# A decoder layer in three-pass fp32r on one core: another order for seven products, background sums on GpSimd's queue, and a norm factor by token columns

## The chip, the core and the metric

The kernel runs on one core of a Trainium2 chip. The metric is device time in microseconds of one execution, inputs and outputs in device memory. All weights and activations are float32.

## What is computed

The reference is one inference step of a one-layer hybrid decoder. A prompt of 1024 tokens and eight samples of 8 tokens each (1088 tokens in all, width 1024) go through the same weights.

```python
def layer(x, ...):
    h = rmsnorm(x, norm_mix)
    q, k, v, gu, gv, ga, gb = split_in(h @ w_in)
    o  = windowed attention with sinks(q, k, v)          # window 128, 16 heads, 4 kv heads
    vn = layernorm(gelu(gv)) ; s = spatial_gating(gelu(gu), vn, ws, bs)
    merged = sigmoid(ga) * (o @ w_pa) + sigmoid(gb) * (s @ w_pb)
    x = x + merged @ w_out
    f, nconv = conv_ffn(rmsnorm(x, norm_ffn), w_up, conv_w, conv_b, w_down, conv_prev)
    return x + f, ...
def conv_ffn(h, w_up, conv_w, conv_b, w_down, prev):
    z = h @ w_up                                          # 1024 -> 2 x 2816
    c = conv_b + sum(concatenate([prev, z])[:, j:j + T] * conv_w[j] for j in range(3))
    a, b = split(c, 2)
    return (gelu(a) * b) @ w_down, ...
```

A final RMSNorm follows; the caches, the last rows of z and the normalised v rows are outputs too.

## The kernel before

**Numbers.** Every float32 operand is split into a high part (rounded to fp32r) and a low part (`split`: ScalarE's copy `wh`, VectorE's difference `wl`), and each product is three fp32r matmuls: high x high, high x low, low x high. So every weight tile costs a load on SyncE's queue (`wraw`), a cast on ScalarE and a subtraction on VectorE before TensorE can use it. The class `Weights` does this: `load` issues the loads in order on SyncE, `emit` the splits some units ahead, `get` hands the next unit to TensorE.

**Stages.** Tokens are columns, in two groups: group 0 has 576 (the samples and 512 of the prompt), group 1 has 512. Both go one after the other through projection, attention (`sc_p`, `tr_p`, `pv_p`, with gate products as filling: `fill`), gated MLP, merge and `w_out` (`x1_tile`, which also sums the squares for the next norm into `nacc` by GpSimd's additions). Group 0 ends at about 479 us of the trace, group 1 at 893. Then come the up-projection with the convolution (893 to 1400) and the down-projection.

**The up-projection by seven products.** For an output block f the two halves of w_up (rows a: a11, a12; rows b: a21, a22, each 512 of the 1024 inputs) and the two halves of the tokens make a 2 x 2 by 2 x 2 product, done with seven products instead of eight. On the weights' side four sums are needed, s1 = a21 + a22, s2 = s1 + a11, s4 = s2 + a12, s3 = a11 + a21 (the tokens' side carries the signs), made by GpSimd (`total`, tiles `ws`); on the tokens' side four differences (`combine`, and `t1_pieces` for group 1). `Chain.product(j, w)` does product j of one group into a PSUM place (`bank`) named by the letter j of `"adadaca"`: place `a` is continued three times, so what stands in it is copied out by ScalarE in between (`keep`: k1, ku, kn), `d` twice, `c` once. `za` and `zb` are the two output blocks.

**Who does what when.** The first FEW = 4 blocks are done for group 0 alone (893 to 953), while the tokens' side of group 1 is made (`rstd_last`, then the pieces of `t1_pieces`). The loop over `order` then does 18 blocks for both groups and, in between, those four for group 1 alone. For the first four blocks the weight sums are made ahead, as a background job in group 1's projection: `weight_sums` loads tiles `hx`, GpSimd adds into `ht`, and the result goes to device memory (`swd`). `half_sums` does the same for group 0's token side in group 1's attention, as an item of `fill` at every third slot (`x1d` in, `t0d` out).

**The order of the work.** The program is written in one order, and a planner (the tile framework) puts each engine's instructions into a queue by its own costs: an instruction that is ready may stand ahead of one that comes before it in the program. On the chip each queue runs strictly in its order. SyncE's queue holds all loads and stores.

Lines the text speaks of: L39 and L40 `split`, L121 the weight load, L151 `total`, L206 `mm3`, L328 and L1003 the reciprocals of the two norms before the up-projection, L348 and L936 the sums of squares, L431 and L451 the background loads, L454 to L457 the weight sums, L458 their store, L496 the scaling of a query tile, L926 `x1_tile`, L1000 to L1003 `rstd_last`, L1067 and L1069 `keep`, L1082 the products, L1093 to L1103 the results, L1110 to L1112 the convolution.

Of the kernel before, what the change touches and what calls it, by code (L numbers as in the profile page):

```python
# [15 lines left out]
P = 128  # L16
# [17 lines left out]
def layer(tc, a):  # L34
# [11 lines left out]
    with ExitStack() as top:  # L46
# [25 lines left out]
        class Weights:  # L72
# [70 lines left out]
            def total(self, name):  # L143

                if name not in self.sums:
# [4 lines left out]
                    t = self.sm.tile([P, 4, P], F32, name="ws", bufs=3)  # L150
                    G.tensor_add(t, x, y)  # L151
# [77 lines left out]
        with ExitStack() as ph1:  # L229
# [135 lines left out]
            for gr in groups:  # L365
# [57 lines left out]
                def half_sums(kk):  # L423
# [3 lines left out]
                    def loads():  # L427
                        x2, t4 = pair_of_tiles()
                        st["x"], st["t"] = x2, t4.rearrange("p (j c) -> p j c", j=4)
                        for e in range(2):  # L430
                            nc.sync.dma_start(x2[:, 576 * e:576 * e + 576], x1d[0][kk + 4 * e])  # L431

                    def sums():
# [6 lines left out]
                        nc.sync.dma_start(t0d[kk][:, 0], halves[0])  # L440
                        nc.sync.dma_start(t0d[kk][:, 1:5], st["t"])
                        nc.sync.dma_start(t0d[kk][:, 5:7], xs[1].rearrange("p (h c) -> p h c", h=2))
                    return loads, sums

                def weight_sums(f, h):

# [3 lines left out]
                    for e in range(2):  # L450
                        nc.sync.dma_start(q[:, e], wt(UP0 + f + e * NFF).rearrange(  # L451
                            "p (q h k) c -> p q h k c", q=2, h=2)[:, :, h])
                    (a11, a12), (a21, a22) = (q[:, 0, 0], q[:, 0, 1]), (q[:, 1, 0], q[:, 1, 1])
                    G.tensor_add(t[:, 0], a21, a22)  # L454
                    G.tensor_add(t[:, 1], t[:, 0], a11)
                    G.tensor_add(t[:, 2], t[:, 1], a12)
                    G.tensor_add(t[:, 3], a11, a21)  # L457
                    nc.sync.dma_start(swd[f][:, :, 2 * h:2 * h + 2], t)  # L458
# [32 lines left out]
                for c in range(2, KD):  # L491
# [8 lines left out]
                    if g == 1:  # L500
                        weight_sums(c // 2 - 1, c % 2)
# [54 lines left out]
                w = W.get()  # L556
                for i, (name, lo) in enumerate(toks):
# [342 lines left out]
                if g == 1:  # L900
                    W.sm = right(tops, "sm")
# [96 lines left out]
        def rstd_last():  # L998
            ps = psu.tile([P, 512], F32, name="st")
            PE.matmul(ps, ones, nacc, start=True, stop=False)  # L1000
            PE.matmul(ps, ones, late["sq"], start=False, stop=True)
            S.activation(nacc, ps, AF.Sqrt, bias=eps, scale=1.0 / D)
            V.reciprocal(nacc, nacc)  # L1003

        def t1_pieces():
# [6 lines left out]
            def norm(k):  # L1012
                V.scalar_tensor_tensor(x1g[k], x1g[k], gains[:, 1, k:k + 1], nacc, ALU.mult, ALU.mult)
# [42 lines left out]
        class Chain:  # L1056
# [15 lines left out]
            def product(self, j, w):  # L1072
                name = "adadaca"[j]
                first = name not in self.bank
                if first:
# [3 lines left out]
                for kk in range(4):  # L1079
                    th, tl = (x[:, (0, 1, 2, 6, 3, 5, 4)[j]] for x in tx[self.g][kk])  # L1080
# [3 lines left out]
                kept = self.kept  # L1084
                if j == 0:
# [3 lines left out]
                elif j == 2:  # L1089
                    self.keep("u", ps)  # L1090
                elif j == 3:
# [292 lines left out]
```

## Time and profile before

| | |
|---|---|
| three runs | 1683.12 us (median), 1682.99, 1685.64 |
| the profiled execution | 1680.17 us, span 1678.5 us, mean granted clock 0.989 |
| TensorE busy | 97% of the span, 10912 matmul records |
| VectorE, ScalarE, GpSimd busy | 62%, 46%, 26% |
| chain that ended last | TensorE 73%, VectorE 9%, GpSimd 6%, DMA 5%, ScalarE 4% |

The profile is one execution; the three runs are others of the same program. "Busy" of TensorE includes matmuls that run at a lowered clock, and matmuls overlap, so the count of matmuls in a window says more than the busy share. In the rows, PE is TensorE, PEld its weight loads, DVE VectorE, ACT ScalarE, POOL GpSimd, SPq SyncE's queue; "x2 | 1.0, 592" is two records, 1.0 us busy, 592 ns each on average; "[1.45 <-ACT kn L1069]" is idle time and what ended it. A row of waits has the time in total, the number of waits and the longest.

### The profile page before, as it was taken

The page shows a single profiled execution, that of the slowest core. Times are in us where ns is not written, and L with a number is a line of the kernel's source. Part 1 is how long each engine was busy: PE and PEld are TensorE (multiplying, and loading weights), DVE is VectorE, ACT ScalarE, POOL GpSimd, SP SyncE. Part 2 cuts the span into 40 slices and gives each one's busy share as a digit, 9 for nine tenths or more (in the row PEclk, how much of TensorE's full clock was granted, in tenths as well). Part 3 has the DMA queues.
Part 4 walks back from the last instruction along what each step waited for, and adds up shares of the span by engine and source line. Part 5 has one row for each costly group of instructions (what it writes and reads, how often), then busy time and mean ns, then how long its engine had stood idle before and what let it go on. Part 6 is the DMA issues. An engine that isn't in the chain of part 4 may idle for free.

```text
span 1678.5 us, 27712 instructions
## 1 busy us (share of the span) xinstructions
PE 1620.8 (97%) x10912; PEld 1507.6 (90%) x10912; DVE 1044.2 (62%) x1437; ACT 773.9 (46%) x1501; POOL 437.1 (26%) x526
## 2 busy tenths in 40 slices
PE   8999999999998999999999999899999999999997
PEld 8989999999976788898878899898998999999886
DVE  8546863644466678565466676868768768355433
ACT  6435653343343465444344555555555546344232
POOL 1302330100451434210012263635536530000001
PEclk9999999999999999999999999999999999999998
DMA  5332223244765522324473523223223227754421
GB/s 191 117 115 80 86 96 119 63 137 145 237 219 187 188 95 94 126 95 129 154 245 125 187 76 111 102 87 115 78 97 101 93 80 239 272 157 133 151 96 55
DMA packets 96179, 221.19 MB, mean 132 GB/s; under 512 B 10416, under 2 KB 24816, under 8 KB 96048
## 3 DMA queue, kind: packets, MB, share of 16 engines
q1 hardware_dynamic: 95904, 219.40, 39.6%
q8 instruction: 86, 1.41, 0.4%
q14 instruction: 45, 0.37, 0.1%
q10 hardware_dynamic: 144, 0.01, 0.0%
HBM read 177.54 MB, written 43.80 MB: 132 GB/s over the span
## 4 chain that ended last, share of the span: by engine, by line
PE 73%; DVE 9%; POOL 6%; DMA 5%; ACT 4%; issue 3%; SPq 1%; DVEq 0%; POOLq 0%; ACTq 0%
PE mm L206 29%; PE st L1082 20%; PE dn L1196 15%; PE mm L552 5%; DVE wl L40 2%; POOL ws L151 2%; DMA wraw<-wt 2%; DMA hx<-wt 1%; PE po L760 1%; PE sc L712 1%; ACT s L727 1%; DVE c L1111 1%; DMA hx<-x1d 1%; ACT wh L39 1%; PE pt L737 1%
## 5 line engine op out<-in xcount | busy, mean ns | idle before, releaser
L206 PE MATMUL mm<-hm,wh 128*128 128x320 f32 (+2 forms) x1920 | 432.5, 333 | 15.6 <-DVE stg L496 6.5
L40 DVE TENSOR_TENSOR wl<-wraw,wh 128x512 fp32r<-128x512 f32 (+3 forms) x314 | 287.9, 932 | 175.6 <-ACT wh L39 171.8
L39 ACT CAST wh<-wraw 128x512 fp32r<-128x512 f32 (+3 forms) x314 | 232.1, 755 | 349.8 <-PE mm L206 120.8
L1082 PE MATMUL st<-th,wh 128*128 128x288 f32 (+1 forms) x1232 | 362.1, 294 | 21.6 <-ACT k L1067 10.9
L1082 PE MATMUL st<-th,wl 128*128 128x288 f32 (+1 forms) x1232 | 359.4, 292 | 2.5 <-DVE wl L40 2.5
L1082 PE MATMUL st<-tl,wh 128*128 128x288 f32 (+1 forms) x1232 | 359.7, 292 | 0.0
L206 PEld LDWEIGHTS mm<-hm,wh 128*128 128x128 f32 x1920 | 303.3, 190 | 46.9 <-issue 8.3
L206 PE MATMUL mm<-hm,wl 128*128 128x320 f32 (+1 forms) x960 | 265.1, 330 | 0.0
L1082 PEld LDWEIGHTS st<-th,wh 128*128 128x128 f32 x1232 | 237.2, 193 | 26.7 <-ACT k L1067 14.0
L1196 PE MATMUL dn<-gr,wh 128*128 128x288 f32 (+3 forms) x1088 | 252.9, 324 | 0.0
L1082 PEld LDWEIGHTS st<-th,wl 128*128 128x128 f32 x1232 | 237.0, 193 | 3.6 <-DVE wl L40 3.5
L1082 PEld LDWEIGHTS st<-tl,wh 128*128 128x128 f32 x1232 | 237.2, 193 | 0.3 <-issue 0.2
L1196 PEld LDWEIGHTS dn<-gr,wh 128*128 128x128 f32 x1088 | 183.1, 188 | 13.9
L1196 PE MATMUL dn<-gr,wl 128*128 128x288 f32 (+3 forms) x544 | 175.8, 323 | 0.0
L206 PEld LDWEIGHTS mm<-hm,wl 128*128 128x128 f32 x960 | 159.6, 190 | 14.5
L1196 PEld LDWEIGHTS dn<-gr,wl 128*128 128x128 f32 x544 | 102.3, 188 | 6.9
L552 PE MATMUL mm<-w2h,hm 128*128 128x256 f32 x576 | 104.6, 283 | 1.7 <-DVE stg L537 1.4
L552 PEld LDWEIGHTS mm<-w2h,hm 128*128 128x128 f32 x576 | 89.8, 191 | 2.4 <-DVE stg L537 1.6
L206 PE MATMUL mm<-qo,wh 128*128 128x320 f32 (+2 forms) x384 | 84.6, 328 | 0.2 <-DVE stg L856 0.2
L552 PE MATMUL mm<-w2l,hm 128*128 128x256 f32 x288 | 81.4, 283 | 0.3 <-DVE w2l L40 0.3
L1111 DVE SCALAR_TENSOR_TENSOR c<-z,cw,c 128x1104 f32<-128x1104 f32 x44 | 71.1, 1620 | 14.6 <-ACT c L1110 14.5
L1229 POOL TENSOR_TENSOR x<-x,rb 128x320 f32<-128x320 f32 (+2 forms) x14 | 12.4, 912 | 260.3 <-PE dn L1196 160.2
(223 smaller groups left out, 2400.9 us busy)
## 6 DMA issues: line engine op xcount, KB each, us to landing
wraw<-wt SPq DMA_DIRECT2D x146, 512.0 KB
wraw<-wt SPq DMA_DIRECT2D x114, 256.0 KB
gd<-z SPq DMA_DIRECT2D x22, 544.0 KB
wraw<-sd SPq DMA_DIRECT2D x32, 256.0 KB
graw<-gd SPq DMA_DIRECT2D x22, 288.0 KB
wraw<-wpb SPq DMA_DIRECT2D x16, 384.0 KB
graw<-gd SPq DMA_DIRECT2D x22, 256.0 KB
gate<-stg SPq DMA_DIRECT2D x16, 288.0 KB
```

What stands on the lines that cost most here:

```text
L39: S.copy(hi, src)
L40: V.tensor_sub(lo, src, hi.bitcast(F32))
L151: G.tensor_add(t, x, y)
L206: PE.matmul(ps[:, lo:lo + c1 - c0], u[:, k, :], v[:, c0:c1], start=(k == 0 and i == 0), stop=(k == nk - 1 and i == 2))
L552: PE.matmul(ps, u[:, lo:lo + P], v[:, k, :], start=(k == 0 and i == 0), stop=(k == KD - 1 and i == 2))
L712: PE.matmul(ps[:, h, o0:256], q, kst[kv][:, e, k0:cur + P], start=e == 0, stop=e == 1)
L727: S.activation(s[:, h], s[:, h], AF.Exp, bias=nm[:, h:h + 1], accum_out=dn[:, h:h + 1])
L737: PE.transpose(pt[:, h * P:h * P + P], s[:, h, 0:P], ident)
L760: PE.matmul(po, vst[b + d][:, kv, :], t, start=e == 0, stop=e == len(parts) - 1)
L1082: PE.matmul(ps, u[:, kk, :], v, start=first and kk + i == 0, stop=kk == 3 and i == 2, skip_group_check=True)
L1111: V.scalar_tensor_tensor(c, z[:, 1:1105], cw[:, i, 1:2], c, ALU.mult, ALU.add)
L1196: PE.matmul(ps, u[:, c, :], v[:, lo:hi], start=f + i == 0, stop=f == NFF - 1 and i == 2, skip_group_check=True)
```

## The change

- **Order of the seven products.** The letters become `"adcadca"`: between two products into the same place stand two others. The weight units follow: a11, s1, a12, s2, s4, a22, s3. Places are started at j = 0, 1, 2 and again, for `c`, at 5. The last two results are now made after product 6: ScalarE copies place `a` negated, VectorE subtracts place `c` from it, GpSimd subtracts k5. Before, ScalarE wrote one of them straight from PSUM and GpSimd the other after product 4. `total("s4")` makes s3 as well, so `ws` has four buffers.
- **Background sums.** The loads of `half_sums` and the loads and the store of `weight_sums` are issued on GpSimd's DMA queue. `weight_sums` gives back its additions as a function, which `next_sums` calls one step later, ahead of the next loads. `half_sums` has its stores as a third item, and `fill` takes an item at every second slot.
- **`rstd_last`.** The sum over the width is taken by token columns (eight matmuls of one column), so square root and reciprocal run on 128 x 4 instead of 128 x 512. Then four matmuls of `ones` with `ident` scaled by a column spread the factors over all partitions again; they stay in PSUM, where `norm` reads them.
- **Memory.** The pools `bt`, `sm` and `w2` change places at the start of block 3 instead of after it.

```diff
@@ total
-                    t = self.sm.tile([P, 4, P], F32, name="ws", bufs=3)
+                    t = self.sm.tile([P, 4, P], F32, name="ws", bufs=4)
                     G.tensor_add(t, x, y)
                     self.sums[name] = t
+                    if name == "s4":
+                        self.total("s3")
@@ emit
-                            src = (lambda: t[:, 0:4], lambda: self.total("s1"),
+                            src = (lambda: t[:, 0:4], lambda: self.total("s1"), lambda: t[:, 4:8],
                                    lambda: self.total("s2"), lambda: self.total("s4"),
-                                   lambda: self.total("s3"), lambda: t[:, 4:8],
-                                   lambda: tb[:, 4:8])[j]()
+                                   lambda: tb[:, 4:8], lambda: self.total("s3"))[j]()
...
-                    for x in (wa[:, 0:4], *(swd[f][:, j] for j in range(4)), wa[:, 4:8], wb[:, 4:8]):
+                    ws = [swd[f][:, j] for j in range(4)]
+                    for x in (wa[:, 0:4], ws[0], wa[:, 4:8], ws[1], ws[2], wb[:, 4:8], ws[3]):
@@ half_sums
-                            nc.sync.dma_start(x2[:, 576 * e:576 * e + 576], x1d[0][kk + 4 * e])
+                            G.dma_start(x2[:, 576 * e:576 * e + 576], x1d[0][kk + 4 * e])
...
-                        nc.sync.dma_start(t0d[kk][:, 0], halves[0])
+
+                    def stores():
+                        nc.sync.dma_start(t0d[kk][:, 0], st["x"][:, 0:288])
                         nc.sync.dma_start(t0d[kk][:, 1:5], st["t"])
...
-                    return loads, sums
+                    return loads, sums, stores
@@ weight_sums
                     for e in range(2):
-                        nc.sync.dma_start(q[:, e], wt(UP0 + f + e * NFF).rearrange(
+                        G.dma_start(q[:, e], wt(UP0 + f + e * NFF).rearrange(
                             "p (q h k) c -> p q h k c", q=2, h=2)[:, :, h])
...
-                    nc.sync.dma_start(swd[f][:, :, 2 * h:2 * h + 2], t)
+                    def sums():
...
+                        G.dma_start(swd[f][:, :, 2 * h:2 * h + 2], t)
+                    return sums
+
+                def next_sums(i):
+                    if g == 1:
+                        if i:
+                            late["sums"]()
+                        late["sums"] = weight_sums(i // 2, i % 2) if i < 2 * FEW else None
...
-                    if g == 1:
-                        weight_sums(c // 2 - 1, c % 2)
+                    next_sums(c - 2)
...
-                    if g == 1:
-                        weight_sums(FEW - 1, kc)
                     w = W.get()
                     ps = acc2()
                     mm3(ps, chunks, w, hs, 0, KD, KD)
+                    next_sums(KD - 2 + kc)
...
                 w = W.get()
+                next_sums(KD)
...
-                    if extra and slots["at"] % 3 == 0:
+                    if extra and slots["at"] % 2 == 0:
...
-                    W.sm = right(tops, "sm")
@@ rstd_last
-            ps = psu.tile([P, 512], F32, name="st")
-            PE.matmul(ps, ones, nacc, start=True, stop=False)
-            PE.matmul(ps, ones, late["sq"], start=False, stop=True)
-            S.activation(nacc, ps, AF.Sqrt, bias=eps, scale=1.0 / D)
-            V.reciprocal(nacc, nacc)
+            ps, rt = psu.tile([P, 512], F32, name="st"), up.tile([P, 4], F32, name="rt", bufs=1)
+            for i in range(4):
+                for x in (nacc, late["sq"]):
+                    PE.matmul(ps[:, i:i + 1], x[:, i * P:i * P + P], ones[:, 0:1], start=x is nacc,
+                              stop=x is not nacc)
+            S.activation(rt, ps[:, 0:4], AF.Sqrt, bias=eps, scale=1.0 / D)
+            V.reciprocal(rt, rt)
+            rs = psu.tile([P, 512], F32, name="st")
+            for i in range(4):
+                S.activation(nacc[:, i * P:i * P + P], ident, AF.Copy, scale=rt[:, i:i + 1])
+                PE.matmul(rs[:, i * P:i * P + P], ones, nacc[:, i * P:i * P + P], start=True, stop=True)
+            return rs
...
-                V.scalar_tensor_tensor(x1g[k], x1g[k], gains[:, 1, k:k + 1], nacc, ALU.mult, ALU.mult)
+                V.scalar_tensor_tensor(x1g[k], x1g[k], gains[:, 1, k:k + 1], rs_last, ALU.mult, ALU.mult)
@@ product
-                name = "adadaca"[j]
-                first = name not in self.bank
-                if first:
+                name = "adcadca"[j]
+                first = j in (0, 1, 2, 5)
+                if name not in self.bank:
...
-                    th, tl = (x[:, (0, 1, 2, 6, 3, 5, 4)[j]] for x in tx[self.g][kk])
+                    th, tl = (x[:, (0, 1, 5, 2, 6, 4, 3)[j]] for x in tx[self.g][kk])
...
                 elif j == 2:
+                    put(self.za, 0, V.tensor_add, kept["1"], ps)
+                elif j == 3:
                     self.keep("u", ps)
...
                 elif j == 4:
+                    put(self.za, 1, V.tensor_add, kept["u"], ps)
+                elif j == 6:
                     self.keep("n", ps, -1.0)
...
-                else:
-                    for to, lo, hi in z_parts(self.zb, self.g, 0):
-                        S.activation(to, pick(ps, to, lo, hi), AF.Copy, scale=-1.0)
+                    put(self.zb, 0, V.tensor_sub, kept["n"], self.bank["c"])
+                    put(self.zb, 1, G.tensor_sub, kept["n"], kept["5"])
@@ the first FEW blocks
         for f in range(FEW):
+            if f == FEW - 1:
+                while rest:
+                    rest.pop(0)()
+                bto.close()
+                W.sm = pool2("sm", 1)
+                W.extend(pool2("w2", 1), 1)
...
-                    rstd_last()
+                    rs_last = rstd_last()
...
-        for go in rest:
-            go()
-        bto.close()
-        W.extend(pool2("w2", 1), 1)
```

More of the change, by code (lines that the diff above doesn't have):

```diff
@@ L439, in sums @@
                         combine(st["t"], *halves)
[L440 removed]
+                    def stores():
+                        nc.sync.dma_start(t0d[kk][:, 0], st["x"][:, 0:288])
                         nc.sync.dma_start(t0d[kk][:, 1:5], st["t"])
[L442 to L443 removed]
+                        nc.sync.dma_start(t0d[kk][:, 5:7], st["x"][:, 576:1152].rearrange(
+                            "p (h c) -> p h c", h=2))
+                    return loads, sums, stores
                 def weight_sums(f, h):
@@ L450, in weight_sums @@
                     for e in range(2):
-                        nc.sync.dma_start(q[:, e], wt(UP0 + f + e * NFF).rearrange(
+                        G.dma_start(q[:, e], wt(UP0 + f + e * NFF).rearrange(
                             "p (q h k) c -> p q h k c", q=2, h=2)[:, :, h])
[L453 to L458, printed above, removed]
+                    def sums():
+                        (a11, a12), (a21, a22) = (q[:, 0, 0], q[:, 0, 1]), (q[:, 1, 0], q[:, 1, 1])
+                        G.tensor_add(t[:, 0], a21, a22)
+                        G.tensor_add(t[:, 1], t[:, 0], a11)
+                        G.tensor_add(t[:, 2], t[:, 1], a12)
+                        G.tensor_add(t[:, 3], a11, a21)
+                        G.dma_start(swd[f][:, :, 2 * h:2 * h + 2], t)
[5 more added lines that the diff above has]
+                        late["sums"] = weight_sums(i // 2, i % 2) if i < 2 * FEW else None
                 def q_tile(c, f):
@@ L1084, in product, with put @@
                 kept = self.kept
+                def put(z, half, op, x, y):
+                    for to, lo, hi in z_parts(z, self.g, half):
+                        op(to, pick(x, to, lo, hi), pick(y, to, lo, hi))
                 if j == 0:
```

8 lines of the change are left out of this document (removed).

## The prediction

> **What bounds the kernel now.** I read the page's busy shares first, then the 40 us windows, then the lists of waits (TensorE, SyncE), then the timelines at the places where the windows sag.
>
> ```profile
> PE 1620.8 (97%) x10912; PEld 1507.6 (90%) x10912; DVE 1044.2 (62%) x1437; ACT 773.9 (46%) x1501; POOL 437.1 (26%) x526
> ```
>
> TensorE is the bound, and the change takes no product away, so a gain can only come from time in which TensorE stands still or runs below its pace. The windows (columns: window, length, busy and count of PE, PEld, DVE, ACT, POOL, granted clock, DMA share, GB/s) show where:
>
> ```profile
> 440.00:480.00 40.00, 36.94 (x271) 35.98 (x270) 12.24 (x11) 13.09 (x20) 26.23 (x24) 1.00 0.75 249
> 960.00:1000.00 40.00, 36.37 (x275) 35.88 (x274) 27.04 (x33) 19.31 (x39) 24.80 (x23) 0.96 0.31 105
> 1000.00:1040.00 40.00, 40.00 (x320) 40.00 (x320) 25.46 (x33) 20.25 (x42) 12.37 (x23) 1.00 0.28 92
> 1040.00:1080.00 40.00, 34.54 (x260) 33.69 (x260) 33.65 (x36) 21.05 (x41) 25.62 (x23) 0.96 0.37 127
> 1160.00:1200.00 40.00, 37.31 (x288) 36.22 (x288) 33.54 (x37) 21.35 (x43) 24.04 (x23) 1.00 0.26 94
> 1240.00:1280.00 40.00, 37.20 (x288) 37.00 (x286) 26.64 (x34) 20.69 (x41) 14.24 (x21) 0.96 0.36 116
> 1280.00:1320.00 40.00, 38.63 (x307) 38.42 (x306) 35.02 (x36) 21.23 (x42) 24.61 (x23) 1.00 0.30 101
> ```
>
> Three stages sag: the start of the second group (440 to 560), the first four output blocks (893 to 953), and the main loop over output blocks (953 to 1400).
>
> **Part 1, the order of the seven products.** An undisturbed window of the main loop holds 320 matmuls, 0.125 us each. The other five lack 45 + 60 + 32 + 32 + 13 = 182, so 22.8 us are lost. TensorE's waits name the cause:
>
> ```profile
> PE st L1082 <- ACT k L1067: 10.9, 10, 2.8
> PE st L1082 <- ACT ku L1067: 5.3, 3, 2.4
> PE st L1082 <- ACT kn L1069: 3.3, 3, 1.4
> 917.34 0.40 PE L1082 MATMUL st<-th,wh 128*128 128x288 f32 x1 [1.45 <-ACT kn L1069]
> 919.89 0.61 PE L1082 MATMUL st<-th,wl 128*128 128x288 f32 x1 [1.88 <-DVE wl L40]
> ```
>
> In sixteen waits, 19.5 us, a matmul that continues a PSUM bank waits until ScalarE has copied the bank out. Three of them lie before 953 (the 1.45 us row and two of about half a microsecond), which leaves 17 us for the main loop. ScalarE is no slow engine (46%); its queue is held:
>
> ```profile
> 1168.24 0.62 ACT L39 CAST wh<-ws 128x512 fp32r<-128x512 f32 x1 [1.41 <-POOL ws L151]
> 1169.88 0.35 ACT L1067 COPY k<-st 128x256 f32<-128x256 f32 x1
> 1170.28 0.39 PE L1082 MATMUL st<-th,wh 128*128 128x256 f32 x1 [1.50 <-ACT k L1067]
> ```
>
> The weight splits stand in ScalarE's queue ahead of the copy and wait for GpSimd's sums. The old order continues bank `a` after one other product. The new one (a d c a d c a) puts two between, and spreads the four sum splits over units 1, 3, 4 and 6 instead of 1 to 4. One product of both groups is 24 matmuls, 24 x 0.125 = 3.0 us, more than the longest wait (2.8). In the four blocks with one chain only it is half of that, so some waits shorten and don't end. I take the 17 us of named idle and leave the other 5.8 (pipeline refill, low clock), for what remains; ends -22.8 and -5 (rival 2).
>
> What it costs: the last result changes from a ScalarE copy to a VectorE subtraction out of PSUM. Its nearest rows are the additions of the same shapes:
>
> ```profile
> 953.20:1400.50 447.30, 430.10 (x3361) 426.40 (x3361) 332.73 (x383) 234.72 (x466) 218.91 (x243) 0.99 0.29 98
> L1100 DVE TENSOR_TENSOR z<-k,st 128x256 f32<-128x256 f32 x22 | 9.2, 417 | 11.4 <-PE st L1082 11.4
> L1100 DVE TENSOR_TENSOR z<-k,st 128x224 f32<-128x224 f32 x18 | 6.8, 379 | 0.0
> L1100 DVE TENSOR_TENSOR z<-k,st 128x64 f32<-128x64 f32 x18 | 3.9, 217 | 23.7 <-PE st L1082 23.7
> ```
>
> That is 9.2 + 6.8 + 3.9 = 19.9 us more for VectorE, which is busy 332.73 of 447.3 us; its 114 us of idle cover it, so zero (without that cover, 19.9). Queued behind the subtraction are weight splits, which here run ahead of their product. GpSimd's subtraction moves from the fifth product to the last; what follows it is the convolution of that block, which TensorE doesn't read. The fourth `ws` buffer is memory only. **Part 1: -17.**
>
> **Part 2, the background sums leave SyncE's queue.** The largest single stall is here. The chain in order of time, then the waits of SyncE (427 to 516) and the clock:
>
> ```profile
> 512.89 0.57 SPq L458
> ...
> 515.21 0.42 SPq L121
> ...
> 515.72 6.07 DMA wraw<-wt
> ...
> 525.59 3.75 DVE nacc L328
> 530.03 1.19 PE L206 MATMUL mm<-hm,wh 128*128 128x512 f32 x2 [6.55 <-DVE stg L496]
> SPq L458 <- POOL ht L456: 34.2, 6, 7.0
> 530.00:532.00 2.00, 1.97 (x5) 1.61 (x6) 1.94 (x3) 1.95 (x3) 0.00 (x0) 0.50 0.02 2
> 532.00:534.00 2.00, 2.00 (x8) 1.57 (x7) 1.97 (x3) 0.24 (x1) 0.00 (x0) 0.71 0.79 260
> ```
>
> SyncE's queue waits for GpSimd's sum to store it (34.2 us in six waits), and the kernel's own weight load at 515.21 stands behind. TensorE idles 6.55 us and then runs four microseconds at 0.50 and 0.71, another 1.0 + 0.6. With loads and stores on GpSimd's queue that weight load can go some 7 us earlier, about the whole stall: -8.1. Next late is the reciprocal (3.75 us) ahead of L496, while TensorE has a second accumulator to fill, so I count nothing for it. The 40 - 36.94 = 3 us idle at 440 to 480 I leave as they are: there the `stg` buffers come free by GpSimd's additions (the L348 row below), and GpSimd gets no faster.
>
> GpSimd pays: 8 steps x 3 issues = 24 DMAs; no row shows one from this queue.
>
> ```profile
> L451 SPq DMA_DIRECT2D hx<-wt x16: 551/616/1020, 427.4 to 505.9; - x16
> 427.00:513.00 86.00, 82.19 (x502) 73.16 (x501) 47.07 (x50) 35.22 (x50) 48.82 (x50) 1.00 0.66 216
> L348 POOL TENSOR_TENSOR pacc<-pacc,stg 128x512 f32<-128x512 f32 x7 | 9.9, 1418 | 0.2
> ```
>
> Bounds: SyncE's 0.616 us for the same transfer, and 6.07 us if the queue were held until a load lands. I take 0.62, the same instruction on another queue: 24 x 0.62 = 15 us, inside GpSimd's idle 86 - 48.8 = 37.2. Behind a waiting sum stand the additions for `nacc` and `pacc`, which free `stg` and feed the second group's norm; that is so today. The row also shows that the planner starts these loads at 427, long before their place in the program, so the new hooks (`next_sums`) fix a dependency more than a time. In attention GpSimd gets eight x1 loads, 8 x 0.62 = 5 us, among masks that TensorE needs: 0 to +5, and as they are spread over the stage I take +1. `stores` one slot later takes SyncE's wait for VectorE away there, worth nothing that TensorE shows. **Part 2: -8 + 1 = -7.**
>
> By the Trainium skill (DMA: Bandwidth & Descriptors, Issuing engines are not separate DMA queues) all issuers share the same DMA engines, and a second one saves only issue time; by that rule this part would be zero (rival 1). The 34.2 us row speaks against it: what is saved is a wait in the queue, not an issue.
>
> **Part 3, rstd_last and the first four blocks.**
>
> ```profile
> 902.00:920.40 18.40, 15.07 (x110) 14.55 (x109) 17.77 (x25) 9.29 (x21) 7.75 (x10) 0.96 0.23 77
> 902.01 3.35 DVE L1003 RECIPROCAL nacc<-nacc 128x512 f32<-128x512 f32 x1
> 577.80 0.18 DVE L729 RECIPROCAL dn<-dn 128x4 f32<-128x4 f32 x1 [1.78 <-ACT s L727]
> 920.00:922.00 2.00, 2.00 (x9) 2.00 (x10) 2.00 (x4) 0.00 (x0) 0.46 (x1) 0.50 0.39 134
> 924.00:926.00 2.00, 1.77 (x8) 1.42 (x6) 1.65 (x4) 1.46 (x4) 1.03 (x1) 0.58 0.89 224
> L1002 ACT ACT_TABLE_LOAD x1 | 1.3, 1283 | 1.1 <-PE st L1001 1.1
> L1000 PE MATMUL st<-nacc,c_ones 128*128 128x512 f32 x2 | 1.0, 592 | 0.0
> L361 PE MATMUL pt<-c_ones,pacc 128*128 128x1 f32 x18 | 2.1, 241 | 0.0
> L737 PE MATMUL pt<-c_ident,s 128*128 128x128 f32 x128 | 19.2, 272 | 0.7 <-DVE s L730 0.6
> ```
>
> VectorE is full here (17.77 of 18.4), and TensorE's two stalls (1.45 + 1.88 = 3.3) and the low clock after them (three windows from 920 to 926, the first and last shown, 0.50, 0.50 and 0.58: 2.8 us) follow from it. The reciprocal falls from 3.35 to 0.18: -3.2 on VectorE; the new subtractions give back 0.6 per block, about 1. Net 2.2 of the 3.3 go, and I take most of the clock loss with them: -5; the two half-microsecond bank waits, -1. New on TensorE (each fp32 matmul stands as two records): eight of one column, 16 x 2.1 / 18 = 1.9, and four of 128, 8 x 19.2 / 128 = 1.2, for two of 512, 2 x 1.0: about +1. The four wait for square root, reciprocal and four ScalarE copies in order; TensorE's queue may stand for the table load (1.3) and as much again, 0 to 3 us, or the planner puts products ahead of them: +1. The earlier close of `bt` and the `sm` and `w2` pools touch nothing that is late: zero, with products of block 3 as cover. **Part 3: -4** (-7 to +3).
>
> **Sum.** -17 - 7 - 4 = -28 on the profiled execution's 1680.17 (span 1678.5): 1652. The median of the runs, 1683.12, lies 2.95 above it, so 1655.
>
> **Rivals.**
> 1. *The queue was not the cause.* Weight loads are late because the DMA engines are busy (share 0.75 at 440 to 480) and stay late. Part 2 gives +1, the sum -20: 1663. Against it: the load was issued late, not only landed late.
> 2. *The wait moves to the weights.* With the banks free, TensorE meets the splits that wait for GpSimd. Part 1 gives -5, the sum -16: 1667. For it: the L39 row above waits 1.41 us for a sum. Against: the sixteen waits name copies only.
> 3. *GpSimd's queue becomes the bound (slower).* Each issue holds GpSimd for x us. Idle covers 37.2 / 24 = 1.55; beyond that `pacc` and the buffers come late by 24x - 37.2, and TensorE's norm with them. Against the other parts' 20 it decides from x = 2.4. At 3.3, the middle of 0.62 and 6.07: 42 - 20 = +22, so 1705. For it: the 26.23 of 40 us GpSimd already works at 440 to 480. Against: at SyncE's issue price there is room. The Trainium skill (SBUF — State Buffer, A bandwidth-pool intuition that's wrong) tells of a transfer from this queue that takes about 3.1 us instead of 0.62 beside a VectorE copy, which would make 1700, as an estimate; no run here shows it yet.
> 4. *It does not do what it says.* The planner rearranges all queues and the waits reappear elsewhere: no change.
>
> **How the numbers follow.** Forecast 0.48, rival 1 0.17, rival 2 0.13, rival 3 0.17, rival 4 0.05. Predicted 1655. The forecast's best end, -22.8 - 8 - 7 and no cost, gives 1645; rivals 1 and 2 together with part 3 at zero give 1680; part of rival 3 and of rival 4 reach 1688. The range is 1644 to 1688, with most of rival 3 left out. 0.2% is 3.4 us, about what a measurement of this kernel can tell from no change. Faster 0.48 + 0.17 + 0.13 = 0.78, same 0.05, slower 0.17.
>
> **What would show it.** Part 1 right: waits on `k`, `ku`, `kn` after the first blocks under 4 us, main loop windows near 320; wrong: waits on `wh`, `wl` or `ws` in their place. Part 2 right: no stall of 6 us between the second group's query products, and SyncE's wait for `ht` gone; wrong: GpSimd's DMA rows longer than 1.55 us, or `pacc` late at the norm. Part 3 right: no reciprocal of 3 us at about 900, and no half clock after it; wrong: a wait of TensorE at the four diagonal matmuls. The prediction as a whole is wrong if the time is over 1680.

## The result, and the profile after

The changed kernel takes 1705.51 us (median of four runs, 1704.60 to 1708.48), the kernel before 1684.38 in the same comparison: a ratio of 1.0127, 95% interval 1.0109 to 1.0145. It is slower by 21 us; the forecast was 1655, the range ended at 1688, and the outcome is rival 3's side and almost its number. The profiled execution took 1708.48 us, the longest of the four; its span is 1706.8. The profile of before is a short execution (1680.17; other runs of that kernel lie between 1678.2 and 1690.8). So the two spans differ by 28 us where the medians differ by 21, and a few microseconds between two traces mean nothing.

Where the time went is seen from the starts of the stages, each the first or last row of its kind in the timeline of TensorE (us):

| | group 0's last product | group 1's values | up-projection | main loop | down-projection | span |
|---|---|---|---|---|---|---|
| before | 477.8 | 548.4 | 893.3 | 954.5 | 1400.3 | 1678.5 |
| after | 509.3 | 576.8 | 928.5 | 986.0 | 1426.5 | 1706.8 |
| part 2 alone (e2) | 510.9 | 578.0 | 927.4 | 987.6 | 1433.6 | 1712.2 |
| parts 1 and 3 (e11) | 478.0 | 553.6 | 897.9 | 952.6 | 1392.2 | 1672.2 |

After is 31 us late by the end of group 0 and 28 to 35 us late until the up-projection; between the starts of the up- and the down-projection it wins 9 back. (Between group 1's values and the first transpose another 6 us are lost, 3.75 of them a wait of the value projection for VectorE that was 1.37 in before; no experiment follows that part.) Busy time by engine, from the page of after, and then its windows in the lost stage, in the columns of before's:

```profile
PE 1626.9 (95%) x10932; PEld 1514.6 (89%) x10932; DVE 1046.5 (61%) x1503; ACT 756.8 (44%) x1439; POOL 445.2 (26%) x558
```

```profile
440.00:480.00 40.00, 23.94 (x152) 23.51 (x151) 5.11 (x5) 7.58 (x11) 22.02 (x26) 0.79 0.47 159
480.00:520.00 40.00, 29.21 (x158) 25.66 (x158) 12.71 (x14) 9.59 (x14) 27.55 (x28) 0.83 0.55 180
```

TensorE's busy time is that of before but for 6 us, so 22 of the 28 us are idle. The first window holds 152 matmuls where before had 271. GpSimd is busy for 22 of 40 us, less than the 26 of before, and the DMA share fell from 0.75 to 0.47: nothing is full, so this is waiting. Who waits for whom (lists of waits of after: TensorE, then GpSimd and SyncE between 425 and 560):

```profile
PE mm L207 <- DVE stg L939: 25.8, 4, 13.1
PE st L1103 <- ACT k L1088: 7.0, 7, 2.2
...
PE st L1103 <- DVE z L1109: 4.5, 3, 1.7
...
POOL hx L457 <- issue: 20.7, 7, 3.7
POOL ht L462 <- DMA hx<-wt: 17.9, 6, 5.9
...
SPq L341 <- POOL nacc L949: 21.9, 3, 7.5
```

The longest of TensorE's waits for L939 can be followed in the timelines of after (GpSimd, then VectorE and TensorE); L457 is the background load, L462 to L465 the sums, L466 their store, L949 the `nacc` addition, L939 `x1_tile`, L341 the load of a piece of x:

```profile
436.81 0.77 POOL L466 DMA_DIRECT2D sd<-ht  x1 [0.42 <-POOL ht L464]
437.51 0.72 POOL L457 DMA_DIRECT2D hx<-wt  x1
441.87 0.72 POOL L457 DMA_DIRECT2D hx<-wt  x1 [3.64 <-issue]
448.51 0.73 POOL L462 TENSOR_TENSOR ht<-hx 128x256 f32<-128x256 f32 x1 [5.92 <-DMA hx<-wt]
...
452.50 0.71 POOL L457 DMA_DIRECT2D hx<-wt  x1
455.52 0.72 POOL L457 DMA_DIRECT2D hx<-wt  x1 [2.31 <-issue]
458.85 0.71 POOL L462 TENSOR_TENSOR ht<-hx 128x256 f32<-128x256 f32 x1 [2.61 <-DMA hx<-wt]
...
460.89 1.39 POOL L949 TENSOR_TENSOR nacc<-nacc,stg 128x576 f32<-128x576 f32 x1
462.31 0.75 DVE L939 TENSOR_TENSOR stg<-stg,mm 128x576 f32<-128x576 f32 x1 [16.51 <-POOL nacc L949]
463.20 1.30 PE L207 MATMUL mm<-hm,wh 128*128 128x320 f32 x4 [13.15 <-DVE stg L939]
```

A store and the first load of the next step go out in 0.7 us each; the second load waits 3.64 us for something the trace does not name ("issue"). Then the queue stands for the landing. The first `nacc` addition stands two such steps behind, amid the sums of a third. It frees the `stg` tile, without which VectorE can't empty TensorE's accumulator. The last two of the four waits go one step further round: the addition that begins at 483.19 frees the tile, SyncE issues the load of x into it at 484.62, and VectorE waits until that has landed. SyncE's 21.9 us for `nacc` (7.8 in before) are waits of this kind. In the timeline of before the same addition started 16 us earlier:

```profile
445.04 1.43 POOL L936 TENSOR_TENSOR nacc<-nacc,stg 128x576 f32<-128x576 f32 x1 [0.45 <-ACT stg L935]
```

### The profile page after: what moved, and what is told of

Its sections match the earlier page's. It is cut to its first block, busy times and chain, and to the rows that moved or that the text cites. A ratio compares the mean times of both kernels' runs of the same rounds, so it can differ in the third digit from the quotient of the medians.

```text
span 1706.8 us, 27748 instructions
## 1 busy us (share of the span) xinstructions
PE 1626.9 (95%) x10932; PEld 1514.6 (89%) x10932; DVE 1046.5 (61%) x1503; ACT 756.8 (44%) x1439; POOL 445.2 (26%) x558
## 4 chain that ended last, share of the span: by engine, by line
PE 67%; DVE 9%; POOL 8%; DMA 6%; issue 5%; ACT 4%; SPq 0%; DVEq 0%; POOLq 0%; ACTq 0%
PE mm L207 26%; PE st L1103 17%; PE dn L1219 15%; PE mm L565 5%; POOL ws L151 2%; DMA wraw<-wt 2%; DVE wl L40 2%; DMA hx<-wt 1%; ACT s L741 1%; PE po L774 1%; PE sc L726 1%; DMA hx<-x1d 1%; ACT wh L39 1%; POOL z L1109 1%; DMA traw<-t0d 1%
## 5 line engine op out<-in xcount | busy, mean ns | idle before, releaser
L207 PE MATMUL mm<-hm,wh 128*128 128x320 f32 (+2 forms) x1920 | 438.0, 337 | 37.7 <-DVE stg L939 25.8
L207 PEld LDWEIGHTS mm<-hm,wh 128*128 128x128 f32 x1920 | 308.4, 193 | 69.4 <-DVE stg L939 13.7
L1132 DVE SCALAR_TENSOR_TENSOR c<-z,cw,c 128x1104 f32<-128x1104 f32 x44 | 66.3, 1508 | 46.6 <-ACT c L1131 46.6
L1131 ACT ACTIVATE c<-z,cw 128x1104 f32<-128x1104 f32 x44 | 57.7, 1311 | 73.0 <-DVE z L1109 40.1
```

The lines of the kernel that those rows point to most:

```text
L207: PE.matmul(ps[:, lo:lo + c1 - c0], u[:, k, :], v[:, c0:c1], start=(k == 0 and i == 0), stop=(k == nk - 1 and i == 2))
L1131: S.activation(c, z[:, 2:1106], AF.Identity, bias=cw[:, i, 3:4], scale=cw[:, i, 2:3])
L1132: V.scalar_tensor_tensor(c, z[:, 1:1105], cw[:, i, 1:2], c, ALU.mult, ALU.add)
```

## The experiments

The theory (Q): GpSimd's in-order queue carries work that TensorE waits for (`nacc`, `pacc`), and part 2 put transfers in front of it that stand. Rivals: the transfers crowd the DMA engines wherever they are issued; the loss comes from the other parts. Every run is given as its ratio to the kernel before, timed beside it, with the run's own median. Differences to the kernel before are the ratio's, times 1684; differences between changed kernels are of medians.

**Which part (e1 to e4, e11).** e1 is the changed kernel with the transfers back on SyncE:

```diff
-                            G.dma_start(x2[...], x1d[0][kk + 4 * e])
+                            nc.sync.dma_start(x2[...], x1d[0][kk + 4 * e])
...
-                        G.dma_start(q[:, e], wt(...)...)
+                        nc.sync.dma_start(q[:, e], wt(...)...)
...
-                        G.dma_start(swd[f][:, :, 2 * h:2 * h + 2], t)
+                        nc.sync.dma_start(swd[f][:, :, 2 * h:2 * h + 2], t)
```

> The changed kernel with all 24 background transfers (loads of half_sums, loads and stores of weight_sums) back on SyncE's queue; everything else as changed, next_sums too. Theory Q (GpSimd's own queue is the cause: it stands while it issues transfers, and the nacc and pacc additions behind it free the stg buffers late): the stall of TensorE behind L939 (25.8 us in the changed kernel) is gone, the stage 440 to 530 is back to its length of before, and what is left is the gain of parts 1 and 3, so 8 to 13 us under the kernel before: 1671 to 1677. Rival T (the transfers themselves, at their new times, crowd the DMA engines, or next_sums moves them to a bad place): the same traffic is still there, so over 1695.

Measured: 0.9938 (0.9916 to 0.9960), 1674.3 us. The 21 us are gone and 10 more.

e2 is the kernel before with the hunks of `half_sums`, `weight_sums`, `next_sums` and `fill` alone:

```diff
-                        weight_sums(c // 2 - 1, c % 2)
+                    next_sums(c - 2)
...
-                        nc.sync.dma_start(q[:, e], wt(...)...)
+                        G.dma_start(q[:, e], wt(...)...)
...
```

> The kernel before with part 2 alone (background transfers on GpSimd's queue, next_sums, half_sums in three items at every second slot). Theory Q: the whole loss is here, without the gain of the other parts: 33 us over the kernel before, 1713 to 1721. Rival (the loss comes from part 1 or 3, or only from all together): 1680 to 1690.

Measured: 1.0166 (1.0146 to 1.0186), 1712.8 us, +28. Part 2 is the loss, a little under the 33 expected.

e3 has the hunks of `total`, `emit`, the weight units and `product`, with the pools of block 3:

```diff
-                name = "adadaca"[j]
+                name = "adcadca"[j]
...
-                    t = self.sm.tile([P, 4, P], F32, name="ws", bufs=3)
+                    t = self.sm.tile([P, 4, P], F32, name="ws", bufs=4)
...
+                W.sm = pool2("sm", 1)
...
```

> The kernel before with part 1 alone (order a d c a d c a, four ws buffers) and the change of pools at block 3 that it needs for its memory. By the prediction's term, -17: 1667. By what the trace of the changed kernel shows of the main loop (waits on k, z, wh and wl are still there in the blocks with one chain), -6 to -9: 1675 to 1678. If part 1 cost as much as it saved: 1684.

Measured: 0.9976 (0.9965 to 0.9986), 1679.7 us. Part 1 is worth 4 us (2 to 6), a quarter of the term and below the second estimate too.

e4 has `rstd_last` and `norm` alone:

```diff
...
-            S.activation(nacc, ps, AF.Sqrt, bias=eps, scale=1.0 / D)
-            V.reciprocal(nacc, nacc)
...
+            S.activation(rt, ps[:, 0:4], AF.Sqrt, bias=eps, scale=1.0 / D)
+            V.reciprocal(rt, rt)
...
-                V.scalar_tensor_tensor(x1g[k], x1g[k], gains[:, 1, k:k + 1], nacc, ALU.mult, ALU.mult)
+                V.scalar_tensor_tensor(x1g[k], x1g[k], gains[:, 1, k:k + 1], rs_last, ALU.mult, ALU.mult)
```

> The kernel before with part 3 alone (rstd_last by token columns). By the prediction's term, -4: 1680. If the shorter reciprocal is given back by the wait for square root, reciprocal and four copies in order: 1684 to 1687.

Measured: 0.9964 (0.9944 to 0.9985), 6 us (3 to 9) faster.

e11 is the changed kernel with everything of part 2 undone:

```diff
-                    next_sums(c - 2)
+                    if g == 1:
+                        weight_sums(c // 2 - 1, c % 2)
...
-                    if extra and slots["at"] % 2 == 0:
+                    if extra and slots["at"] % 3 == 0:
...
```

> The kernel before with parts 1 and 3 and nothing of part 2 (weight_sums, its places and half_sums as before). If next_sums and the three items of half_sums are worth nothing once the transfers are on SyncE's queue, the same as the changed kernel with that queue, 1674 (1671 to 1677), which is also the sum of the two parts alone (4.7 + 6.4 = 11). If they are worth something: 1678 to 1683.

Measured: 0.9955 (0.9938 to 0.9971), 1674.2 us. Within these intervals the parts add up, and `next_sums` without its queue is worth nothing that can be told apart from e1.

**What the "issue" waits are (e5, e13).** e5 changes one number; GpSimd's instructions stand in exactly the order of the changed kernel.

```diff
-                   dynamic_dma_scratch_size=1024)
+                   dynamic_dma_scratch_size=4096)
```

> The changed kernel with four times the memory for the descriptors that GpSimd writes for its transfers (dynamic_dma_scratch_size 4096 instead of 1024); GpSimd's instructions stand in nearly the same order. Theory R (the 2.3 to 3.7 us before every second background load, 20.7 us in seven waits that nothing in the trace explains, are a full ring: store and loads of a step don't fit into it together): these waits vanish, and the time falls to 1685 to 1692, as the waits for the landing of hx (17.9 us) stay. Rival F (a fixed price of a transfer on this queue, which the next one has to wait out): the waits stay at 2 to 4 us and the time at 1703 to 1709.

Measured: 1.0039 (1.0024 to 1.0055), 1690.6 us, 15 less than the changed kernel. The timeline of GpSimd in e5, and two rows of its waits (GpSimd's and TensorE's, 425 to 560):

```profile
441.15 0.76 POOL L466 DMA_DIRECT2D sd<-ht  x1 [0.30 <-POOL ht L464]
441.85 1.42 POOL L457 DMA_DIRECT2D hx<-wt  x2
449.37 0.73 POOL L462 TENSOR_TENSOR ht<-hx 128x256 f32<-128x256 f32 x1 [6.10 <-DMA hx<-wt]
```

```profile
POOL ht L462 <- DMA hx<-wt: 27.7, 8, 6.1
PE mm L207 <- DVE stg L939: 18.3, 4, 9.1
```

Both loads go out in one piece and the 20.7 us are gone: what GpSimd waited for was room for the descriptors that it writes for its transfers. Part of what they cost reappears as landing (17.9 to 27.7), and TensorE still waits 18.3 us for L939.

e13 gives half of that room:

```diff
-                   dynamic_dma_scratch_size=1024)
+                   dynamic_dma_scratch_size=2048)
```

> The changed kernel with dynamic_dma_scratch_size 2048 instead of 1024 (4096 gave 1690.6). GpSimd's instructions stand in the same order. If twice the room is enough for the store and two loads of a step, the waits before the second load vanish and the time is that of 4096, 1687 to 1694. If a step needs more than twice, they stay in part: 1697 to 1706.

Measured: 1.0047 (1.0030 to 1.0063), 1691.3 us, as e5. Twice the room is enough.

**Only some of the transfers moved (e6, e7).** e6 puts the store back on SyncE, e7 all loads:

```diff
# e6
-                        G.dma_start(swd[f][:, :, 2 * h:2 * h + 2], t)
+                        nc.sync.dma_start(swd[f][:, :, 2 * h:2 * h + 2], t)
# e7
...
-                        G.dma_start(q[:, e], wt(...)...)
+                        nc.sync.dma_start(q[:, e], wt(...)...)
```

> The changed kernel with the store of weight_sums on SyncE's queue; the loads stay on GpSimd's. Theory R (ring full): without the store in it the two loads find room, the waits of 2.3 to 3.7 us before the second load vanish; the landing waits stay, SyncE waits for GpSimd's sums again: 1690 to 1698. Rival F (fixed price): the second load still waits over 2 us, 1700 to 1708.

> The changed kernel with all background loads on SyncE's queue; only the store of weight_sums stays on GpSimd's, where it follows the sums that make it. Theory Q and R: one issue of under 1 us per step and no wait for room: 1672 to 1680, and if SyncE's queue loses its wait for ht so that the weight load goes early, the stall of 7.6 us at L511 goes too: 1666. Rival F: each store holds GpSimd some 3 us, 8 x 3 = 24 us: 1685 to 1695.

Measured: e6 1.0125 (1.0098 to 1.0152), e7 0.9997 (0.9984 to 1.0011). Both expectations of theory R were missed, e6 by 8 us, e7 by 3; e6 has the time that rival F gave, but not by its reason. Waits of e6 between 425 and 560 (GpSimd, SyncE, TensorE):

```profile
POOL ht L462 <- DMA hx<-wt: 32.7, 8, 6.5
SPq L466 <- POOL ht L464: 49.4, 7, 8.6
PE mm L207 <- DVE stg L939: 28.7, 6, 8.0
```

The wait for room did vanish, as theory R said, but nothing was won: GpSimd stands for the landing instead, and SyncE stands again for the sums. And e7, with one transfer of 0.73 us per step on GpSimd and no wait for room, is still 9 us over e1. Its timeline shows what is left: the planner has strung the additions between the sums of later steps, so that they wait with them.

```profile
469.79 0.73 POOL L462 TENSOR_TENSOR ht<-hx 128x256 f32<-128x256 f32 x1 [3.07 <-DMA hx<-wt]
470.49 1.29 POOL L350 TENSOR_TENSOR pacc<-pacc,stg 128x512 f32<-128x512 f32 x1
471.74 0.73 POOL L463 TENSOR_TENSOR ht<-ht,hx 128x256 f32<-128x256 f32 x1
472.42 1.27 POOL L350 TENSOR_TENSOR pacc<-pacc,stg 128x512 f32<-128x512 f32 x1
```

In before and in e1 whole steps and batches of up to six additions take turns, and the first batch follows the second step. So part of the loss is the order in which the planner lays GpSimd's queue once a transfer is in it; how much, no run separates.

**The additions out of the queue (e8, e9).** In e8 all transfers stay on GpSimd and the additions leave it; e9 has the larger memory too.

```diff
-                    G.tensor_add(acc, acc, sq)
+                    V.tensor_add(acc, acc, sq)
...
-                        G.tensor_add(nacc, nacc, sq)
+                        (G if g else V).tensor_add(nacc, nacc, sq)
# e9 too
-                   dynamic_dma_scratch_size=1024)
+                   dynamic_dma_scratch_size=4096)
```

> The changed kernel with the nacc and pacc additions of group 0's end (15 of 128x512 and 128x576) on VectorE instead of GpSimd; all background transfers stay on GpSimd's queue. Theory Q (the transfers hurt because these additions stand behind them and free stg late): the waits of 25.8 us on L939 go below 6 us and the time to 1672 to 1682, although GpSimd's own waits stay as long. Rival T (crowded DMA engines, or the late weight loads themselves): xt and weights still come late, 1695 to 1705.

> The changed kernel with both mendings together: group 0's nacc and pacc additions on VectorE, and four times the descriptor memory. All background transfers stay on GpSimd's queue. With the additions moved alone, GpSimd's steps ended so late that VectorE stood 16 us for the x1 loads (L439) and TensorE 14.1 us behind it. Theory Q with R: without the full ring a step is some 2.5 us shorter, 8 x 2.5 = 20 us, so that wait goes and nothing of part 2's loss is left: 1664 to 1671. Rival (VectorE pays for the additions, or the wait for landing alone is enough to hold it): 1676 to 1682.

Measured: e8 0.9969 (0.9954 to 0.9984), 1679.2 us, 26 under the changed kernel although GpSimd's own waits got no shorter (19.3 us for room, 34.1 for landing; 20.7 and 17.9 in after): theory Q is shown, and crowded DMA engines are out. TensorE's wait on L939 is gone, but there is a new one (timelines of VectorE and TensorE, e8):

```profile
540.38 1.55 DVE L439 SCALAR_TENSOR_TENSOR hx<-hx,c_gains,nacc 128x576 f32<-128x576 f32 x2 [16.03 <-DMA hx<-x1d]
544.56 1.19 PE L207 MATMUL mm<-hm,wh 128*128 128x512 f32 x2 [14.09 <-DVE stg L511]
```

GpSimd's steps end so late that the x1 load behind them is late, VectorE stands for it, and TensorE for VectorE. With room for the descriptors (e9) that goes as well: 0.9922 (0.9907 to 0.9937), 1669.0 us. Its lists of waits, TensorE and, between 500 and 560, VectorE:

```profile
PE mm L565 <- DVE stg L550: 3.9, 1, 3.9
PE mm L207 <- DVE stg L939: 3.3, 3, 1.9
...
DVE hx L439 <- DMA hx<-x1d: 2.7, 2, 1.5
```

**The best versions (e10, e12, e14).** e10 is e1 with the additions on VectorE; e12 is the kernel before with that move alone; e14 is e10 with two `hx` buffers and the loads a step earlier:

```diff
# e10, e12, e14
-                    G.tensor_add(acc, acc, sq)
+                    V.tensor_add(acc, acc, sq)
...
# e14 too
-                    return (kvp.tile([P, 1152], F32, name=x) for x in ("hx", "ht"))
+                    return (kvp.tile([P, 1152], F32, name=x, bufs=b) for x, b in (("hx", 2), ("ht", 1)))
...
-                        if i:
-                            late["sums"]()
-                        late["sums"] = weight_sums(i // 2, i % 2) if i < 2 * FEW else None
+                        new = weight_sums(i // 2, i % 2) if i < 2 * FEW else None
+                        if i:
+                            late["sums"]()
+                        late["sums"] = new
```

> The changed kernel with all background transfers on SyncE's queue and group 0's nacc and pacc additions on VectorE: the version that parts 1 and 3 and the finding on the additions point to. The waits of 5.5 us on L939 go; the stall of 7.6 us at L511 stays if it hangs on SyncE's order (the weight load behind the store of the sums): 1668 to 1672; if GpSimd, done earlier, also frees SyncE: 1661 to 1667. If the additions cost VectorE as much: 1674 to 1680.

> The kernel before with one edit: group 0's nacc and pacc additions on VectorE. If the 6 us that this move brought beside parts 1 and 3 are its own, 1676 to 1679; if they need the rest of the change, 1681 to 1685.

> As e10 (background transfers on SyncE, additions on VectorE, 1668.5), with two hx buffers and each step's loads issued ahead of the sums of the step before. If SyncE's queue stands because the next loads wait for the single hx, GpSimd's waits for landing (47 us) and the 3.6 us stall at L511 go: 1662 to 1666. If what holds SyncE is the store that waits for the sums (39.9 us), which this leaves in place: 1667 to 1671.

Measured: e10 0.9918 (0.9903 to 0.9934), 1668.5 us; e12 0.9973 (0.9959 to 0.9988), 4.5 us under before; e14 0.9889 (0.9871 to 0.9907), 1666.1 us, the lowest median. e12 says that most of what the additions bring was to be had without the change. e9 and e10 come out alike: once nothing of TensorE's stands behind the transfers and there is room for them, no difference shows between the two queues. In e14 no wait for `stg` of L511 is left in TensorE's list (e10: 3.6 us), and SyncE's wait for the sums fell from 39.9 to 28.7 (waits of SyncE and TensorE in e14, whose L940 is L939 elsewhere):

```profile
SPq L466 <- POOL ht L464: 28.7, 7, 7.0
PE mm L207 <- DVE stg L940: 4.7, 3, 2.1
```

e14 and e10 were each compared with before, not with each other, and their intervals overlap, so that e14 is the faster of the two isn't shown.

## Why the prediction was wrong

**Part 2, the step that failed: "24 x 0.62 = 15 us, inside GpSimd's idle 86 - 48.8 = 37.2".** It has two errors. The price was nearly right for the issue alone (0.72 for a load, 0.76 for the store); the second load of a step waited for room on top (20.7 us in seven waits), which the range from 0.62 to 6.07 contained and the chosen value did not. The larger error is the cover. The list of waits of before shows of what those 37.2 us were made:

```profile
POOL ht L454 <- DMA hx<-wt: 26.3, 6, 6.8
POOL nacc L936 <- ACT stg L935: 6.1, 5, 2.6
POOL ht L454 <- issue: 3.1, 1, 3.1
```

26.3 us are waits for a load to land, 3.1 more stand before a sum with no releaser named, and 6.1 are waits for the squares. So most of this idle lies within the chain of load, sum and store that the transfers belong to. A transfer that must follow the sums and precede the next sums can't lie in the wait for itself; it lengthens the chain. The sentence on the additions behind a waiting sum, "that is so today", was true of the instructions and false of the order: in before two steps stood ahead of the first addition, in after most of a third as well, with 3.64 + 2.31 us for room and another landing.

Rival 3 had the place (`pacc` and buffers late) and the total (1705), but its number is right partly by accident. Worked out from the trace, issues and waits for room make (16 x 0.72 + 8 x 0.76 + 20.7) / 24 = 1.6 us per transfer, under its deciding point of 2.4; by its formula the kernel would have come out faster. It counted GpSimd's idle as room, as the forecast did.

The rule of the Trainium skill that I weighed (DMA: Bandwidth & Descriptors, Issuing engines are not separate DMA queues) gave zero for the part; e9 against e10 agrees with it, where no work that TensorE needs stands behind the transfers and there is room for them. The same page of the Trainium skill, SWDGE vs HWDGE vs iDMA, says that GpSimd builds its descriptors in software into rings kept in a part of SBUF, and assigns plain transfers to SyncE or ScalarE; e5 and e13 change nothing but the room for descriptors, and the 20.7 us of waits go. The slow transfer beside a VectorE copy that I quoted from the Trainium skill (SBUF — State Buffer, A bandwidth-pool intuition that's wrong) was not put to the test: every GpSimd issue of a weight load in after took 0.712 to 0.894 us, but between 425 and 527 VectorE ran no plain copy, only operations with two tensor inputs.

The reading of the 6.55 us stall is supported and not shown. With the store off SyncE's queue it is gone (0.2 us in after, none in e7 and e9, against 7.6 in e1). But e10 and e12, where SyncE waits as long for the sums (39.9 and 40.1 us, 34.2 in before), keep only 3.6 and 3.7 of it, so the additions on GpSimd had a part in it too. And its end brought nothing: e9 is no faster than e10, since 3.9 us at the value projection follow in e9 (1.2 in e10): something else was late next.

The term of +1 for the attention stage held: from the first transpose to the up-projection it lasts 320 us in before, 321 in after (worked out from the timelines).

**Part 1: -17 expected, -4 measured (2 to 6).** The mechanism is there: waits on `ku` and `kn` are gone, and in the main loop's blocks with both chains TensorE's idle falls from 10.4 us (before) to 4.3 (e11), both summed from the timelines. The failed step is "One product of both groups is 24 matmuls, 24 x 0.125 = 3.0 us, more than the longest wait (2.8)", from which all 17 us of the main loop's waits were taken, though the next sentence excepts the blocks with one chain. In those four blocks the waits rose from 6.6 to 8.9 us, and 2.5 came new at the start of the down-projection, so that idle fell by 1.5 in all; the rest of the 6 us by which the main loop is shorter is pace (TensorE is busy 428.6 us for 3349 matmuls in before and 424.0 in e11, the granted clock 0.99 and 1.00). TensorE in the timeline of e11, where L1091 is the products, L1076 `keep`, L1097 the results:

```profile
1045.98 0.38 PE L1091 MATMUL st<-th,wh 128*128 128x256 f32 x1 [2.24 <-ACT k L1076]
1145.33 0.39 PE L1091 MATMUL st<-th,wh 128*128 128x256 f32 x1 [1.65 <-ACT k L1076]
1270.52 0.38 PE L1091 MATMUL st<-th,wh 128*128 128x256 f32 x1 [1.67 <-DVE z L1097]
1392.23 0.85 PE L1207 MATMUL dn<-gr,wh 128*128 128x288 f32 x2 [2.49 <-DVE z L1097]
```

The rows with `z` are new: place `c` is started a second time, so it waits for VectorE's addition out of it, and both of a block's last results now come after product 6. I costed VectorE's work at zero by its idle share (114 us) without asking who waits for it. A second step failed with it: "what follows it is the convolution of that block, which TensorE doesn't read". ScalarE begins that convolution (L1119), and a later copy `k` stands behind it in ScalarE's queue. ScalarE in e11, its list of waits between 952.6 and 1392.2 and its timeline:

```profile
ACT c L1119 <- POOL z L1097: 31.7, 16, 4.8
...
1044.36 1.31 ACT L1119 ACTIVATE c<-z,cw 128x1104 f32<-128x1104 f32 x1 [2.21 <-POOL z L1097]
...
1143.01 0.62 ACT L39 CAST wh<-ws 128x512 fp32r<-128x512 f32 x1 [2.33 <-POOL ws L151]
```

In before ScalarE has no wait for GpSimd's `z` in the main loop. The copies that free TensorE at 1045.98 and 1145.33 begin at 1045.58 and 1144.92, the first behind the convolution that waits for the moved subtraction, the second behind a weight split that waits for a sum, and a convolution. How much of part 1's missing gain this is, no run separates. Rival 2 (waits on `wh` and `wl`) shows in e11's main loop for 1.5 us only; its -5 is nearer to the measured size than my term, for another reason.

**Part 3: -4 expected, -6 measured (3 to 9).** The size agrees. VectorE and TensorE in the timeline of after show the steps as told: a short reciprocal, and no wait at the four matmuls of the diagonals (two records each).

```profile
935.48 0.18 DVE L1019 RECIPROCAL rt<-rt 128x4 f32<-128x4 f32 x1 [0.45 <-ACT rt L1018]
937.75 0.78 PE L1023 MATMUL st<-nacc,c_ones 128*128 128x128 f32 x4
938.50 0.61 PE L1023 MATMUL st<-nacc,c_ones 128*128 128x128 f32 x4
```

But the place of the gain was not as told. The first four blocks as one window each, in the columns of before's windows: before, e3 (part 1), e4 (part 3), e11 (both).

```profile
893.26:954.47 61.21, 54.25 (x353) 51.18 (x352) 42.41 (x70) 31.56 (x66) 15.69 (x23) 0.92 0.50 155
```

```profile
898.99:959.25 60.26, 51.60 (x353) 48.71 (x352) 44.61 (x77) 30.95 (x59) 13.98 (x21) 0.97 0.48 148
```

```profile
899.71:960.59 60.88, 54.77 (x373) 52.92 (x372) 37.58 (x70) 32.26 (x70) 14.86 (x23) 0.92 0.48 156
```

```profile
897.85:952.55 54.70, 52.22 (x374) 50.74 (x373) 38.94 (x76) 31.08 (x62) 11.54 (x20) 0.97 0.51 164
```

Each part alone leaves them at 60 to 61 us in its trace. All eleven traces of kernels with both parts are shorter, 54.7 to 57.5 us (57.5 in that of the changed kernel); the five with one or none lie between 59.4 and 61.2. With part 3 alone another wait for a weight split comes just before the same half clock (TensorE's timeline and one window of e4):

```profile
931.31 0.61 PE L1090 MATMUL st<-th,wl 128*128 128x288 f32 x1 [3.31 <-DVE wl L40]
```

```profile
932.00:934.00 2.00, 2.00 (x10) 2.00 (x10) 2.00 (x5) 0.00 (x0) 0.00 (x0) 0.50 0.77 276
```

Where e4 alone gained its 6 us can't be told from its trace, which is of an execution (1682.31 us) 4 us longer than its median.

## What to carry to other kernels

Before work is moved to an engine because it is idle, list what that idle is made of: idle that waits inside the same chain is no room, and everything behind it in the queue waits longer. A transfer put on a compute engine's queue is priced by the steps that it holds back and who needs them, not by its issue time; the cheap test is to take the needed work out of that queue (e8) or to give the transfers room (e5). And where a reordering lengthens the cover of a wait, look at the blocks with the least cover first: the waits moved there.

## What the runs showed of the hardware

- A background transfer issued by GpSimd shows as 0.56 us (x1 load), 0.72 (weight load) or 0.76 (store), medians in after. With `dynamic_dma_scratch_size` at 1024, the second load after a store then waited 2.3 to 3.7 us with no releaser in the trace; at 2048 and 4096 the wait is gone (e13, e5), and so it is at 1024 without the store in that queue (e6).
- A stalled TensorE also lost pace: the granted clock was 0.79 and 0.83 in the two windows from 440 to 520, where before showed 1.00 in both.
